# Shifting the weight pieces that stream through TensorE by 48 bytes against their activations

## The chip, the core and the metric

The kernel runs on one core of a Trainium2 chip. The metric is device time in microseconds (us) of one execution. All matrix work is on TensorE (PE), which loads a stationary operand of up to 128x128 (the profile's engine PEld) and then streams a moving operand through the array (PE). VectorE (DVE) and ScalarE (ACT) prepare operands, SyncE (SP) issues the DMAs.

## The reference

Two layers of a decoder trunk over one sequence of 256 tokens, width 2048, all in float32. Every sub-layer is a modulation of its input, a mixer or MLP, a gated residual and a layer norm:

```python
for layer in range(DEPTH):                      # DEPTH = 2
    h = x * (1.0 + scale[:, 0, None]) + shift[:, 0, None]
    y = rglru_mixer(h, ...) if mixer == 0 else nsa_mixer(h, ...)
    x = _layer_norm(DN_ALPHA * x + (1.0 + gate[:, 0, None]) * y, ...)
    h = x * (1.0 + scale[:, 1, None]) + shift[:, 1, None]
    y = jnp.square(jax.nn.relu(h @ w1)) @ w2    # w1: 2048 x 8192, w2: 8192 x 2048
    x = _layer_norm(DN_ALPHA * x + (1.0 + gate[:, 1, None]) * y, ...)
```

Layer 0 mixes with a gated linear recurrence (`lru`), layer 1 with block-sparse attention (`nsa`). Scale, shift and gate come from the matrix `ada_w`. Nearly all of the time is in products of 256 token rows with large weight matrices that are read once from HBM.

## The kernel before, in words

A float32 product is made of three float32r matmuls: every operand is split into a high part (rounded to float32r by a ScalarE copy) and a low part (the rest, by a VectorE subtraction), and `mm3` (lines 208 to 212) issues high x high on line 210, high x low on line 211 and low x high on line 212, into one PSUM bank.

Weights come as a stream of 1 MB items. `prefetch` keeps up to six of them in flight in the tile `raw`. `pump` splits an item, two pieces of 512 columns at a time, into the rings `whi` and `wlo` (lines 143 and 144). Each ring has 16 pieces of 2048 bytes per partition; a split waits until the ring has room, that is until `take` has counted old pieces as consumed. Items of kind "a" (`ada_w`) go through the same stream and are reduced by VectorE on line 125.

A piece is used in one of two ways:

- **weights stationary** (`gemm_ws`, `gemm_ws_outer`, and the small product for the attention gates, lines 1075 to 1087): a 128-column slice of the piece is loaded, and 256 columns of activations move. In the trace these are the rows `128*128 128x256` with `g<-s,whi` or `m<-s,whi`; the moving operand is named first. The attention gates load 48 columns at a time, `128*48`.
- **weights moving** (`gemm_as`): a 128x128 block of activations is loaded, and the whole piece, 512 columns, moves. These are the rows `128*128 128x512` with `g<-whi,s` or `g<-wlo,s`. They are the output products of both mixers (384 matmuls each), every `w2` product of the two MLPs (4 times 384 each), and three single products: two value projections of the attention (96 each) and the first quarter of the first `w1` product of layer 1 (96). That makes 384 + 4x384 + 2x96 + 384 + 96 + 4x384 = 4128 matmuls.

The order of the moving products in time is: mixer output of layer 0 (from 297 us), MLP of layer 0 (from 498, 676, 853 and 1028 us), two value projections (after the norm at 1115 us), mixer output and first `w1` quarter of layer 1 (from 1412 us), MLP of layer 1 (from 1624, 1799, 1974 and 2149 us).

Where the operands lie within a partition follows from the sizes of the tiles in their order of allocation: `whi` begins at byte 50304 and `wlo` at byte 83072, both 128 modulo 256, and every piece and every 128-column slice is a multiple of 256 bytes from there. The activations' high and low parts are slices of 4096-byte tiles (`s` in the trace) from byte 146240 on; each of them begins at 64 modulo 256. So where weights move, the moving operand lies 128 - 64 = 64 bytes past the stationary one, modulo 256; where activations move, 64 - 128 = 192. Only the attention gates differ: their stationary slices step by 192 bytes and so pass through 128, 64, 0 and 192. In the attention and in the recurrence gates there are also matmuls on plain float32 operands, which appear as two records each.

Of the kernel before, what the change touches and what calls it, by code (L numbers as in the profile page):

```python
# [10 lines left out]
F32R = mybir.dt.float32r  # L11
# [18 lines left out]

RAW = 6
RING = 16
NS4 = 20
NS2 = 6
LNACT = (0, 2)
# [5 lines left out]
class Item:  # L41
    def __init__(self, kind, src, col=None, then=None, width=2048):
        self.kind, self.src, self.col, self.then, self.width = kind, src, col, then, width
        self.group = 0
        self.done = False
        self.run = None
        self.pieces = {"w": width // 512, "g": 2}.get(kind, 0)


class Builder:  # L50
    def __init__(self, ctx, tc, a, out):
        self.tc, self.nc, self.a, self.out = tc, tc.nc, a, out
        nc = self.nc
        self.const = ctx.enter_context(tc.tile_pool(name="const", bufs=1))
        self.pool = ctx.enter_context(tc.tile_pool(name="work", bufs=1))
        self.psum = ctx.enter_context(tc.tile_pool(name="psum", bufs=1, space=PSUM))
        self.dram = ctx.enter_context(tc.tile_pool(name="dram", bufs=1, space=DRAM))
        self.raw = self.const.tile([128, RAW, 2048], F32, name="raw")
        self.whi = self.const.tile([128, RING, 512], F32R, name="whi")
        self.wlo = self.const.tile([128, RING, 512], F32R, name="wlo")  # L60
        self.now = 0.0
        self.tasks = []
        self.items = []
        self.di = self.pi = 0
        self.cons = self.prod = 0
        self.slot = self.inflight = 0
        self.hold = self.calm = False
        self.behind, self.left = [], 0
        self.arrive = []
        self.uid = 0  # L70


    def t4(self, shape, dtype=F32):
        self.uid += 1
        return self.pool.tile(shape, dtype, name=f"s{self.uid}", tag="s4", bufs=NS4)

# [11 lines left out]

    def set_stream(self, items):
        self.items = items  # L90
        p = 0
        for it in items:
            it.p0 = p
            p += it.pieces
        self.prefetch()

    def prefetch(self):
# [13 lines left out]
    def pump(self):  # L111
        nc = self.nc
        while self.pi < len(self.items):
            it = self.items[self.pi]
            if it.kind == "d":
                self.pi += 1
                continue
            if self.hold or self.arrive[self.pi] > self.now:
                return
            r = it.raw  # L120
            if it.kind == "a":
                if self.calm:
                    return
                with self.queue():
                    nc.vector.scalar_tensor_tensor(r, r, self.one, self.cond, op0=OP.mult, op1=OP.mult, accum_out=it.col)  # L125
            elif it.kind == "raw":
                if not it.run(r):
                    return
            elif it.kind == "p":
                it.run(r)  # L130
            elif it.kind == "n":
                if not it.done:
                    return
            else:
                w = min(1024, it.width)
                s = it.p0 + 2 * it.group
                if s + 2 > self.cons + RING:
                    return
                src = r[:, 1024 * it.group:1024 * it.group + w]
                hi = self.whi[:, s % RING:s % RING + 2, :].rearrange("p a b -> p (a b)")[:, :w]  # L140
                lo = self.wlo[:, s % RING:s % RING + 2, :].rearrange("p a b -> p (a b)")[:, :w]
                with self.queue():
                    nc.scalar.activation(hi, src, AF.Copy)  # L143
                    nc.vector.tensor_tensor(out=lo, in0=src, in1=hi.bitcast(F32), op=OP.subtract)  # L144
                self.prod = s + 2
                it.group += 1
                if 2 * it.group < it.pieces:
                    continue
            self.pi += 1
            self.inflight -= 1  # L150
            self.prefetch()
            if it.then:
                it.then()
# [41 lines left out]

    def piece(self, i):
        self.until(lambda: self.prod > i)
        return self.whi[:, i % RING, :], self.wlo[:, i % RING, :]

    def take(self):  # L200
        self.cons += 1

    def head(self, kind):

        self.until(lambda: self.items[self.pi].kind == kind and not self.items[self.pi].done and self.arrive[self.pi] <= self.now)
        return self.items[self.pi], self.items[self.pi].raw
# [92 lines left out]
def build(ctx, tc, a, out):  # L299
    B = Builder(ctx, tc, a, out)  # L300
# [46 lines left out]
    def ada_items(s, part, tiles=range(16), then=None):  # L347
        its = [Item("a", a["ada"][s, part * 16 + k], col=mods[s][:, part * 16 + k:part * 16 + k + 1]) for k in tiles]
        if then:
            its[-1].then = then  # L350
        return its
# [6 lines left out]
    def W(name, *ix):  # L358
        return Item("w", a[name][ix])

    def N(name, *ix):
        return Item("n", a[name][ix])

    def merge(main, side):
        res, j = [], 0
        for i, m in enumerate(main):
            res.append(m)
            while j < len(side) and (j + 1) * len(main) <= (i + 1) * len(side):
                res.append(side[j])
                j += 1  # L370
        return res + side[j:]
# [3 lines left out]
    def hook(key):  # L375
        return lambda: hooks[key]()
# [52 lines left out]
    lru_in = [N("lru_gate", 0), N("lru_gate", 1)]  # L429
    for c in (2, 3):  # L430
        lru_in += [W("lru_in", 4 + c, g) for g in range(4)] + [W("lru_in", c, g) for g in range(4)] + [N("lru_gate", c)]
    lru_out = [W("lru_out", n, g) for n in range(4) for g in range(4)]
    def ss_group(k0, k1):
        ks = range(k0, k1)
        return ada_items(1, 0, ks) + ada_items(1, 1, ks, hook(("h1", k0, k1)))
# [9 lines left out]
    def mlp_items(l):  # L445
        its = []
        for q in range(4):
            its += [W("mlp_w1", l, 4 * q + i, g) for i in range(4) for g in range(4)]
            its += [W("mlp_w2", l, n, 4 * q + g) for n in range(4) for g in range(4)]
        return its  # L450

    m0 = mlp_items(0)
    stream += merge(m0[16:], ada_items(1, 2, then=hook(("gate", 1))) + ada_items(2, 0) + ada_items(2, 1, then=hook(("ss", 2))) + ada_items(2, 2, then=hook(("gate", 2))))
    nsa = []
    for ch in (4, 5, 0, 1, 2, 3):
        if ch == 4 or ch == 5:
            idx = {4: 3, 5: 5}[ch]
        else:
            idx = (0, 1, 2, 4)[ch]
        nsa += [W("nsa_kv", idx, g) for g in range(4)]  # L460
    nsa.append(Item("g", a["nsa_g"], width=768))
    cmp_raw = [Item("raw", a["cmp_w1"][i]) for i in range(4)]
    q_items = [W("nsa_q", c, g) for c in range(4) for g in range(4)]
    for i, at in enumerate((18, 21, 24, 27)):
        nsa.insert(at, cmp_raw[i])
    nsa += q_items + [W("nsa_out", n, g) for n in range(4) for g in range(4)]
    stream += merge(nsa, ada_items(3, 0) + ada_items(3, 1, then=hook(("ss", 3))))
    m1 = mlp_items(1)
    stream += m1[:16] + merge(m1[16:96], ada_items(3, 2, then=hook(("gate", 3)))) + m1[96:]

# [606 lines left out]
    gbank = B.bank([128, 256], "g")  # L1077
    whi, wlo = B.piece(B.cons)
    B.until(lambda: B.prod > B.cons + 1)
    ghi = B.whi[:, B.cons % RING:B.cons % RING + 2, :].rearrange("p a b -> p (a b)")  # L1080
    glo = B.wlo[:, B.cons % RING:B.cons % RING + 2, :].rearrange("p a b -> p (a b)")
    for k in range(NK):
        ahi, alo = act(k)
        B.mm3(gbank[0:48, :], ghi[:, 48 * k:48 * k + 48], glo[:, 48 * k:48 * k + 48], ahi, alo, k == 0, k == NK - 1)
# [223 lines left out]
```

## Time and profile before

| | us |
|---|---|
| median of 3 runs | 2252.34 (2247.26 to 2256.88) |
| the profiled execution, its own time | 2251.0 |
| its span, first to last instruction | 2249.2 |
| PE busy | 2152.1 (96% of the span) |
| weight loads (PEld) busy | 1923.5 (86%) |
| DVE busy | 1634.6 (73%) |
| ACT busy | 1058.0 (47%) |

A matmul's duration in the profile runs from its issue to the end of its drain, so consecutive matmuls overlap in the rows; what one costs in a dense stretch is the distance from its start to the next one's. "Granted clock" is the share of TensorE's 2.4 GHz that the chip let through: 1.00 is 2.4 GHz, 0.50 is 1.2 GHz. At 2.4 GHz, 256 columns take 106.7 ns and 512 columns 213.3 ns.

### The profile page before, as it was taken

The page shows a single profiled execution, that of the slowest core. Times are in us where ns is not written, and L with a number is a line of the kernel's source. Part 1 is how long each engine was busy: PE and PEld are TensorE (multiplying, and loading weights), DVE is VectorE, ACT ScalarE, POOL GpSimd, SP SyncE. Part 2 cuts the span into 40 slices and gives each one's busy share as a digit, 9 for nine tenths or more (in the row PEclk, how much of TensorE's full clock was granted, in tenths as well). Part 3 has the DMA queues.
Part 4 walks back from the last instruction along what each step waited for, and adds up shares of the span by engine and source line. Part 5 has one row for each costly group of instructions (what it writes and reads, how often), then busy time and mean ns, then how long its engine had stood idle before and what let it go on. Part 6 is the DMA issues. An engine that isn't in the chain of part 4 may idle for free.

```text
span 2249.2 us, 34081 instructions
## 1 busy us (share of the span) xinstructions
PE 2152.1 (96%) x14093; PEld 1923.5 (86%) x14093; DVE 1634.6 (73%) x1959; ACT 1058.0 (47%) x1387; POOL 0.2 (0%) x4
## 2 busy tenths in 40 slices
PE   3799999899999999999999999999999999999997
PEld 3698877898998898898789998788989989988986
DVE  8888888797677676868898688768777554555566
ACT  2355563554544354354353355536544544543541
POOL 0000000000000000000000000000000000000000
PEclk9899999999999999999999999999999999999999
DMA  9988879699888887879599876355888655555671
GB/s 393 414 316 348 337 294 355 263 344 381 321 306 299 303 324 285 317 291 354 198 345 349 341 274 256 108 206 189 290 326 304 217 191 188 197 197 188 213 255 38
DMA packets 98775, 625.02 MB, mean 278 GB/s; under 512 B 10963, under 2 KB 13443, under 8 KB 27452
## 3 DMA queue, kind: packets, MB, share of 16 engines
q1 hardware_dynamic: 98620, 622.85, 74.0%
q8 instruction: 110, 1.80, 0.3%
q14 instruction: 45, 0.37, 0.0%
HBM read 614.36 MB, written 8.45 MB: 277 GB/s over the span
## 4 chain that ended last, share of the span: by engine, by line
PE 84%; DVE 8%; ACT 3%; DMA 2%; issue 2%; SPq 0%; DVEq 0%; ACTq 0%
PE g L211 26%; PE g L212 26%; PE g L210 26%; DVE raw L125 3%; DVE wlo L144 2%; ACT whi L143 1%; DMA raw<-in_lru_in 1%; PE m L1156 1%; PE m L1190 1%; DMA raw<-in_ada 1%; PE g L896 0%; PE m L1182 0%; PE m L398 0%; DMA raw<-in_cmp_w 0%; PE m L1193 0%
## 5 line engine op out<-in xcount | busy, mean ns | idle before, releaser
L144 DVE TENSOR_TENSOR wlo<-raw,whi 128x1024 fp32r<-128x1024 f32 x721 | 868.8, 1222 | 432.6 <-ACT whi L143 431.1
L143 ACT ACTIVATE whi<-raw 128x1024 fp32r<-128x1024 f32 x721 | 753.4, 1057 | 833.4 <-PE g L212 411.3
L210 PE MATMUL g<-s,whi 128*128 128x256 f32 (+1 forms) x2768 | 771.6, 280 | 60.3 <-ACT s L548 59.1
L211 PE MATMUL g<-s,whi 128*128 128x256 f32 (+1 forms) x2768 | 771.3, 279 | 3.2 <-DVE s L549 3.2
L212 PE MATMUL g<-s,wlo 128*128 128x256 f32 (+1 forms) x2768 | 770.7, 279 | 2.3 <-DVE wlo L144 2.3
L210 PEld LDWEIGHTS g<-s,whi 128*128 128x128 f32 (+1 forms) x2768 | 522.4, 189 | 73.3 <-ACT s L548 60.1
L210 PE MATMUL g<-whi,s 128*128 128x512 f32 x1376 | 540.9, 394 | 5.4 <-ACT whi L143 3.4
L211 PE MATMUL g<-wlo,s 128*128 128x512 f32 x1376 | 542.2, 394 | 2.9 <-DVE wlo L144 2.9
L212 PE MATMUL g<-whi,s 128*128 128x512 f32 x1376 | 542.1, 395 | 0.0
L212 PEld LDWEIGHTS g<-s,wlo 128*128 128x128 f32 (+1 forms) x2768 | 522.8, 189 | 6.6 <-DVE wlo L144 5.5
L211 PEld LDWEIGHTS g<-s,whi 128*128 128x128 f32 (+1 forms) x2768 | 523.6, 189 | 5.7 <-DVE s L549 4.7
L125 DVE SCALAR_TENSOR_TENSOR raw<-raw,one,cond 128x2048 f32<-128x2048 f32 x176 | 411.5, 2346 | 62.3 <-DMA raw<-in_ada 61.6
L210 PEld LDWEIGHTS g<-whi,s 128*128 128x128 f32 x1376 | 259.1, 188 | 65.7 <-ACT whi L143 4.3
L211 PEld LDWEIGHTS g<-wlo,s 128*128 128x128 f32 x1376 | 259.2, 188 | 62.9 <-DVE wlo L144 3.9
L212 PEld LDWEIGHTS g<-whi,s 128*128 128x128 f32 x1376 | 259.3, 188 | 55.8 <-DVE s L549 0.9
L210 PE MATMUL m<-s,whi 128*128 128x256 f32 x256 | 70.6, 277 | 0.2 <-ACT whi L143 0.2
L212 PE MATMUL m<-s,wlo 128*128 128x256 f32 x256 | 70.7, 277 | 0.0
L211 PE MATMUL m<-s,whi 128*128 128x256 f32 x256 | 70.7, 277 | 0.0
L507 ACT ACTIVATE s<-s,hB,hA 128x256 f32<-128x256 f32 x32 | 16.7, 592 | 101.3 <-DVE hA L483 75.7
L549 DVE TENSOR_TENSOR s<-t,s 128x512 fp32r<-128x512 f32 x78 | 53.3, 685 | 3.4 <-ACT s L548 3.2
L731 ACT ACTIVATE t<-g 128x512 f32<-128x512 f32 x58 | 34.0, 587 | 33.2 <-PE g L212 33.2
L548 ACT ACTIVATE s<-t 128x512 fp32r<-128x512 f32 x78 | 47.7, 622 | 2.5 <-DVE t L616 2.3
(196 smaller groups left out, 1045.0 us busy)
## 6 DMA issues: line engine op xcount, KB each, us to landing
raw<-in_mlp_w SPq DMA_DIRECT2D x256, 1024.0 KB
raw<-in_ada SPq DMA_DIRECT2D x176, 1024.0 KB
raw<-in_lru_in SPq DMA_DIRECT2D x28, 1024.0 KB
raw<-in_nsa_kv SPq DMA_DIRECT2D x24, 1024.0 KB
raw<-in_gate SPq DMA_DIRECT2D x16, 1024.0 KB
raw<-in_lru_out SPq DMA_DIRECT2D x16, 1024.0 KB
raw<-in_nsa_q SPq DMA_DIRECT2D x16, 1024.0 KB
raw<-in_nsa_out SPq DMA_DIRECT2D x16, 1024.0 KB
```

Source lines behind the costliest of these rows:

```text
L125: nc.vector.scalar_tensor_tensor(r, r, self.one, self.cond, op0=OP.mult, op1=OP.mult, accum_out=it.col)
L143: nc.scalar.activation(hi, src, AF.Copy)
L144: nc.vector.tensor_tensor(out=lo, in0=src, in1=hi.bitcast(F32), op=OP.subtract)
L210: mm(out, lhi, rhi, start=start, stop=False, skip_group_check=True)
L211: mm(out, lhi, rlo, start=False, stop=False, skip_group_check=True)
L212: mm(out, llo, rhi, start=False, stop=stop, skip_group_check=True)
L507: SC.activation(x[:, j, :], x[:, j, :], AF.Identity, scale=hA[s][:, k:k + 1], bias=hB[s][:, k:k + 1])
L548: SC.activation(hi, src, AF.Copy)
L549: V.tensor_tensor(out=lo, in0=src, in1=hi.bitcast(F32), op=OP.subtract)
L731: SC.activation(r2, banks[b], AF.Relu)
L1156: T.matmul(ps, qT[:, h, 128 * t:128 * t + 128], kT[g // 2][:, g % 2, :, 0:K], start=True, stop=True)
L1190: T.matmul(po, vt[br][:, kt, 128 * g:128 * g + 128], pT[:, br, kt], start=first, stop=False)
```

## The change

Both rings become flat tiles of 16 x 512 elements and 64 elements (256 bytes) of room. A piece whose item is marked as moving is stored 12 elements (48 bytes) from the tile's start plus its slot; every other piece lies 64 elements (256 bytes) from there, which is where it was, modulo 256. The tiles behind the rings move by 512 bytes, so they too keep their places modulo 256. For the moving pieces the distance from moving to stationary operand goes from 64 to 112, modulo 256; nothing else changes its distance.

A moving piece therefore overlaps the last 208 bytes of the slot ahead of it. Two rules keep this safe: at each passage from ordinary to moving pieces two slots are skipped (`skip`, stepped over in `take`), and `pump` doesn't split into ordinary slots until the moving piece that ends in them has been consumed. The matmuls, their order and their operands' values stay as they are.

```diff
 RING = 16
+PLACE = 64
+AHEAD = 52
...
-        self.whi = self.const.tile([128, RING, 512], F32R, name="whi")
-        self.wlo = self.const.tile([128, RING, 512], F32R, name="wlo")
+        self.whi = self.const.tile([128, 512 * RING + PLACE], F32R, name="whi")
+        self.wlo = self.const.tile([128, 512 * RING + PLACE], F32R, name="wlo")
...
     def set_stream(self, items):
         self.items = items
-        p = 0
+        p, last, row = 0, False, -1
         for it in items:
+            if it.pieces and it.moving and not last:
+                self.skip |= {p, p + 1}
+                p += 2
+                row += 1
             it.p0 = p
-            p += it.pieces
+            for _ in range(it.pieces):
+                self.off[p] = PLACE - AHEAD if it.moving else PLACE
+                p += 1
+            if it.pieces:
+                last = it.moving
         self.prefetch()
...
                 if s + 2 > self.cons + RING:
                     return
+                old = s + 2 - RING
+                if not it.moving and old >= self.cons and self.off.get(old, PLACE) != PLACE:
+                    return
                 src = r[:, 1024 * it.group:1024 * it.group + w]
-                hi = self.whi[:, s % RING:s % RING + 2, :].rearrange("p a b -> p (a b)")[:, :w]
-                lo = self.wlo[:, s % RING:s % RING + 2, :].rearrange("p a b -> p (a b)")[:, :w]
+                o = self.off[s] + 512 * (s % RING)
+                hi, lo = self.whi[:, o:o + w], self.wlo[:, o:o + w]
...
     def piece(self, i):
         self.until(lambda: self.prod > i)
-        return self.whi[:, i % RING, :], self.wlo[:, i % RING, :]
+        o = self.off[i] + 512 * (i % RING)
+        return self.whi[:, o:o + 512], self.wlo[:, o:o + 512]
 
     def take(self):
         self.cons += 1
+        while self.cons in self.skip:
+            self.cons += 1
...
-    lru_out = [W("lru_out", n, g) for n in range(4) for g in range(4)]
+    lru_out = moving([W("lru_out", n, g) for n in range(4) for g in range(4)])
...
-            its += [W("mlp_w2", l, n, 4 * q + g) for n in range(4) for g in range(4)]
+            its += moving([W("mlp_w2", l, n, 4 * q + g) for n in range(4) for g in range(4)])
+        if l == 1:
+            moving(its[:4])
         return its
```

The same mark is put on the items of the two value projections and of `nsa_out`, and the small product for the attention gates reads its two pieces at `PLACE`.

## Rows read from the trace of the kernel before

**Rows 1.** The page, busy time by engine: us, share of span, instructions.

```profile
PE 2152.1 (96%) x14093; PEld 1923.5 (86%) x14093; DVE 1634.6 (73%) x1959; ACT 1058.0 (47%) x1387; POOL 0.2 (0%) x4
```

**Rows 2.** The page, the chain that ended last: share of the span by engine.

```profile
PE 84%; DVE 8%; ACT 3%; DMA 2%; issue 2%; SPq 0%; DVEq 0%; ACTq 0%
```

**Rows 3.** PE groups by line and shape: count | busy us, mean ns | idle before.

```profile
L210 PE MATMUL g<-s,whi 128*128 128x256 f32 x2752 | 767.1, 280 | 60.3 <-ACT s L548 59.1 <-ACT whi L143 1.2
...
L211 PE MATMUL g<-wlo,s 128*128 128x512 f32 x1376 | 542.2, 394 | 2.9 <-DVE wlo L144 2.9
L212 PE MATMUL g<-whi,s 128*128 128x512 f32 x1376 | 542.1, 395 | 0.0
L210 PE MATMUL g<-whi,s 128*128 128x512 f32 x1376 | 540.9, 394 | 5.4 <-ACT whi L143 3.4 <-ACT s L548 2.1
```

**Rows 4.** Timeline of PE from 1974 us, weights moving: start us, duration us.

```profile
1973.77 0.39 PE L210 MATMUL g<-whi,s 128*128 128x512 f32 x1
...
1989.79 0.39 PE L211 MATMUL g<-wlo,s 128*128 128x512 f32 x1
```

**Rows 5.** The same from 525 us, weights moving.

```profile
525.11 0.40 PE L210 MATMUL g<-whi,s 128*128 128x512 f32 x1
...
535.84 0.40 PE L212 MATMUL g<-whi,s 128*128 128x512 f32 x1
```

**Rows 6.** The same from 1905 us, activations moving.

```profile
1904.75 0.28 PE L210 MATMUL g<-s,whi 128*128 128x256 f32 x1
...
1912.91 0.28 PE L210 MATMUL g<-s,whi 128*128 128x256 f32 x1
```

**Rows 7.** The same from 655 us, activations moving.

```profile
654.77 0.28 PE L211 MATMUL g<-s,whi 128*128 128x256 f32 x1
...
662.89 0.28 PE L211 MATMUL g<-s,whi 128*128 128x256 f32 x1
```

**Rows 8.** Timeline of PE and PEld together, weights moving.

```profile
1974.00 0.39 PE L211 MATMUL g<-wlo,s 128*128 128x512 f32 x1
1974.00 0.19 PEld L212 LDWEIGHTS g<-whi,s 128*128 128x128 f32 x1
1974.22 0.39 PE L212 MATMUL g<-whi,s 128*128 128x512 f32 x1
1974.23 0.19 PEld L210 LDWEIGHTS g<-whi,s 128*128 128x128 f32 x1
```

**Rows 9.** Timeline of PE from 1269 us, attention gates, 48 columns loaded each.

```profile
1268.78 0.28 PE L210 MATMUL g<-s,whi 128*48 128x256 f32 x1
...
1274.10 0.28 PE L212 MATMUL g<-s,wlo 128*48 128x256 f32 x1
```

**Rows 10.** The chain in order of time, recurrence gates (float32): start, us, what.

```profile
227.82 1.73 PE m L896 x8
229.55 1.73 PE g L896 x8
231.28 1.73 PE m L896 x8
```

**Rows 11.** Busy time by window: PE, PEld, DVE, ACT, POOL, clock, DMA share, GB/s.

```profile
56.00:112.00 56.00, 39.91 (x309) 38.93 (x308) 49.55 (x52) 21.20 (x26) 0.00 (x0) 0.85 1.01 415
...
300.00:380.00 80.00, 80.00 (x342) 65.52 (x343) 74.00 (x81) 33.88 (x34) 0.00 (x0) 0.98 0.91 349
500.00:585.00 85.00, 85.00 (x366) 68.86 (x365) 63.43 (x58) 39.45 (x49) 0.00 (x0) 1.00 0.93 363
680.00:762.00 82.00, 82.00 (x353) 66.39 (x353) 60.04 (x55) 31.46 (x31) 0.00 (x0) 1.00 0.82 306
...
1805.00:1885.00 80.00, 80.00 (x351) 65.66 (x350) 39.19 (x36) 31.07 (x30) 0.00 (x0) 1.00 0.56 190
```

**Rows 12.** ACT's longest waits by line: us in total, times, longest.

```profile
ACT whi L143 <- PE g L212: 411.3, 253, 11.3
ACT whi L143 <- PE g L211: 320.5, 208, 3.1
```

**Rows 13.** The chain in order of time, ahead of the first MLP.

```profile
458.06 8.47 DMA raw<-in_ada
...
466.55 2.37 DVE raw L125 x2
```

More of the change, by code (lines that the diff above doesn't have):

```diff
@@ L47, in __init__, with moving @@
         self.pieces = {"w": width // 512, "g": 2}.get(kind, 0)
+        self.moving = False
+def moving(items):
+    for it in items:
+        it.moving = True
+    return items
 class Builder:
@@ L66, in __init__ @@
         self.slot = self.inflight = 0
+        self.skip, self.off = set(), {}
         self.hold = self.calm = False
@@ L459, in build @@
             idx = (0, 1, 2, 4)[ch]
-        nsa += [W("nsa_kv", idx, g) for g in range(4)]
+        its = [W("nsa_kv", idx, g) for g in range(4)]
+        nsa += moving(its) if ch in (4, 5) else its
     nsa.append(Item("g", a["nsa_g"], width=768))
@@ L465, in build @@
         nsa.insert(at, cmp_raw[i])
-    nsa += q_items + [W("nsa_out", n, g) for n in range(4) for g in range(4)]
+    nsa += q_items + moving([W("nsa_out", n, g) for n in range(4) for g in range(4)])
     stream += merge(nsa, ada_items(3, 0) + ada_items(3, 1, then=hook(("ss", 3))))
@@ L1079, in build @@
     B.until(lambda: B.prod > B.cons + 1)
-    ghi = B.whi[:, B.cons % RING:B.cons % RING + 2, :].rearrange("p a b -> p (a b)")
-    glo = B.wlo[:, B.cons % RING:B.cons % RING + 2, :].rearrange("p a b -> p (a b)")
+    go = PLACE + 512 * (B.cons % RING)
+    ghi, glo = B.whi[:, go:go + 1024], B.wlo[:, go:go + 1024]
     for k in range(NK):
```

## The prediction

> **What bounds the kernel now.** I read the page first: PE is busy for 96% of the span [rows 1] and holds 84% of the chain that ended last [rows 2], so time is won or lost on PE. Then I grouped PE's work by shape. Idle time ahead of the 512-column groups is at most 5.4 us a line [rows 3], and in the windows that lie wholly in such work PE is busy all the time [rows 11]. What matters there is the distance between one matmul and the next, which the durations in a group don't show. So I took start times.
>
> Weights moving, from 1973.77 to 1989.79 us there are 71 starts, 70 steps in 16.02 us: **228.9 ns** a step [rows 4]. From 525.11 to 535.84 us there are 47 starts: 10.73/46 = **233.3 ns** [rows 5]. Activations moving: 73 starts, 8.16/72 = **113.3 ns** [rows 6], and elsewhere 70 starts, 8.12/69 = **117.7 ns** [rows 7]. So each shape has a narrow and a wide spacing, both 4.4 ns apart, at the full 2.4 GHz (granted clock 1.00 [rows 11]) and with no change of the addresses modulo 256. The wide one holds in the first two MLP products of layer 0, from 498 and 676 us: 768 matmuls; 366 matmuls in 85 us and 353 in 82 us [rows 11] agree with it, as 351 in 80 us do with the narrow one (a window also counts a matmul or two that straddle its edges). The other 3360 of the 4128 moving-weight matmuls I take as narrow.
>
> Against streaming alone (213.3 ns for 512 columns, 106.7 for 256) the excess is 15.6 or 20.0 ns with moving weights, and 6.6 or 11.0 with moving activations. Beside every matmul a load for the next one runs; it starts with the matmul, at 1974.00 and at 1974.23 against 1974.22 [rows 8]. So two reads of SBUF run side by side, and the change alters their distance modulo 256 for the moving weights alone, from 64 to 112.
>
> **What the moving pieces may gain.** No row has a float32r matmul at a distance that isn't a multiple of 64, so the cost at 112 can't be read; I bound it.
>
> The best end: the float32 matmuls of the recurrence gates stream 256 columns twice in a record, 512 column times, beside a load of 128 columns, and 24 records in 5.19 us take 216.2 ns each [rows 10]. That is 2.9 ns above the 213.3, with no visible price for the load. It would save 228.9 - 216.2 = 12.7 ns a narrow and 17.1 ns a wide matmul.
>
> The value I take is nearer: moving activations in the narrow spacing, which are of the same type. Their 6.7 ns above streaming looks like a fixed price of a float32r matmul, for the attention gates keep it while they load only 48 columns and pass through the distances 192, 0, 64 and 128: 48 starts, 5.32/47 = 113.2 ns [rows 9]. If loading cost something there, a load of a third of the length should be cheaper. With the same price a 512-column matmul stands at 213.3 + 6.7 = **220.0 ns**. The two observed values are then two and three steps of 4.4 ns above it (228.9 and 233.3), and the wide moving activations one step above 113.3. I read the steps as collisions of the two reads, and forecast that the new distance removes them where weights move: 8.9 ns a narrow matmul, 13.3 a wide one.
>
> The worst end: one step is added, as rows 5 have against rows 4: 4.4 ns x 4128 = 18 us of loss. Two steps, as far as the narrow spacing lies above 220.0, would be 37 us.
>
> **Where the gain arrives.** The mixer output of layer 0 (384 matmuls from 297 us) is followed by a norm and by a stage whose chain runs over a DMA of `ada_w` of 8.47 us and its reductions [rows 13]; what PE wins ahead of that it waits for there. I count these 384 at nothing (3.4 us if the stage doesn't hold it back). All later products are followed by PE-bound work. The sum: 768 x 13.3 = 10.2 us, and (3360 - 384) x 8.9 = 26.5 us; together **36.7 us**.
>
> **The other parts of the edit.** The two skipped slots shorten the split's lead from 16 to 14 pieces at each passage to moving weights. A piece is worth 6 x 228.9 = 1.37 us of PE, so the lead falls from about 22 to 19 us. ACT's split waits for PE to free slots for 411.3 + 320.5 us [rows 12], so the ring is full most of the time and 2.7 us less lead is covered; without that cover it would be 2.7 us at each of ten passages, 27 us. The extra wait for an ordinary piece behind moving ones holds it back by one consumed piece, 1.37 us, under the same cover. Behind a split that has to wait stand the VectorE reductions of line 125 and, through `raw`, SP's next DMAs; those are the queues to look at. The two-halves products, which need all 16 pieces at once, follow other moving pieces or begin after a passage, so no skip falls within their 16. ACT and DVE write the same sizes to other addresses; I count nothing. The DMA has to follow: the busiest window with moving weights, 500 to 585 us, has a DMA share of 0.93 at 363 GB/s; 233.3/220.0 of it is 385 GB/s, under the 415 seen at 56 to 112 us [rows 11]. A shortfall would cost a few us there.
>
> So 2251.0 - 36.7 = 2214.3 us for the profiled execution; the median of the runs is 1.3 us above that execution, so **2215 us** (-1.7%).
>
> **A rule against it.** The load and the stream run side by side in rows 8, and the excess in rows 4 and 5 is what I ascribe to their meeting. The Trainium skill, "TensorE: Matmul & The Clock Gate", section "Part 2: What happens when you issue a matmul", says that PE has two independent SBUF read ports, so that loading the next weights doesn't take read bandwidth from the running matmul. By that rule an address can't matter, and the sum would be zero, not 36.7. The trace agrees with it in rows 10, and rows 9 show no effect of distance or load length; rows 4 to 7 show that something other than streaming costs 4.4 ns at a time, which the rule doesn't explain.
>
> **Rivals.**
> 1. *The distance doesn't matter.* The excess belongs to the float32r stream or to the hand-over between matmuls; the narrow and wide spacings would be a timing relation that sets itself. For it: the spacing changes at equal addresses, and rows 9 have one spacing at four distances. Against it: moving activations show that a float32r matmul beside a full load can do with 6.7 ns, where moving weights pay 15.6. Time: 2251, within 2240 to 2263. A change that fails to move the pieces as it says would look the same.
> 2. *Part of it.* One of two steps goes: 4.4 x 3744 = 16.6 us, 2235.
> 3. *Slower: the new place makes the reads meet more often.* Before, every operand starts on a multiple of 64 bytes; after, the moving ones start 48 past one. If a read that straddles two such blocks occupies both, each matmul gets one step more: 233.3 where it was 228.9, 237.8 where it was 233.3. That is 18 us, 2269 to 2271; with two steps 2289. It decides as soon as the steps gained by the distance are fewer than those lost to the straddling.
>
> **How the numbers follow.** The forecast with all that lies down to the best end, 2194 to 2226 us (the low end: 2976 x 12.7 + 768 x 17.1 = 50.9 us, and 384 x 12.7 = 4.9 us if the first product's gain arrives too): 0.46. Part of it, 2226 to 2240: 0.13. No effect: 0.22. Slower: 0.19. A measurement of this kernel tells about 0.5% (11 us) from no change, so faster 0.59, same 0.22, slower 0.19. The range of 2194 to 2262 us leaves the slower case out. Cases of one sign hold most; the likeliest one's own range is 2194 to 2226.
>
> **What would show it.** Right: steps of about 220 ns in the 512-column stretches, 113.3 ns unchanged where activations move, and 512-column products of 384 matmuls in about 84.5 us instead of 87.9 or 89.6. The forecast is wrong if they stay at 228.9 and 233.3 (rival 1), go to 224 to 229 (rival 2) or rise (rival 3); the covers are wrong if PE waits for lines 143 or 144 at the passages to moving weights, or if the stage after a product gives the gain back in waits for DMA. The wide spacing can also come and go in other stretches: every hundred matmuls in it with moving activations cost 0.44 us.

## The result, and the profile after

The changed kernel took **2266.36 us** (2265.78 to 2266.96) against 2251.98 us (2247.26 to 2256.88) of the kernel before: ratio **1.0072**, 95% interval 1.0058 to 1.0087. It is 0.7% slower where 1.7% faster was forecast, and outside the range. The profiled execution took 2265.78 us with a span of 2264.0, 14.8 us more than the span before.

The page of the kernel after, its busy times and its chain by engine, as in [rows 1, 2]:

```profile
PE 2170.5 (96%) x14093; PEld 1940.3 (86%) x14093; DVE 1637.4 (72%) x1959; ACT 1059.5 (47%) x1387; POOL 0.2 (0%) x4
...
PE 85%; DVE 8%; DMA 3%; ACT 2%; issue 2%; SPq 0%; DVEq 0%; ACTq 0%
```

PE is busy for 18.4 us more, with the same 14093 instructions; the chain is PE's as before. So matmuls became dearer, and no other engine got in the way. The longest waits of ACT's split, and those of PE for the two split lines (now 167 and 168; `mm3` is on 237 to 239), say the same. Columns: us in total, times, longest.

```profile
ACT whi L167 <- PE g L239: 404.2, 246, 12.1
ACT whi L167 <- PE g L238: 338.2, 206, 3.2
...
PE g L237 <- ACT whi L167: 4.3, 3, 3.4
PE g L238 <- DVE wlo L168: 2.9, 2, 1.6
PE g L239 <- DVE wlo L168: 2.3, 4, 0.7
```

PE's waits for the split in the kernel before, where the split lines were 143 and 144:

```profile
PE g L210 <- ACT whi L143: 4.6, 3, 3.4
...
PE g L211 <- DVE wlo L144: 2.9, 2, 1.6
PE g L212 <- DVE wlo L144: 2.3, 4, 0.7
```

ACT waits 742.4 us for PE, against 731.8 [rows 12]: the ring is as full as it was. PE waits 4.3, 2.9 and 2.3 us for the split, against 4.6, 2.9 and 2.3 before.

Which matmuls? Windows of 80 us that lie wholly inside one kind of work, first three of the kernel before, then four of the kernel after. The count behind PE's busy time is the reading: 80 us divided by it (less one or two that straddle the edges) is the step from one matmul to the next.

```profile
857.00:937.00 80.00, 80.00 (x352) 65.62 (x351) 60.41 (x57) 31.15 (x30) 0.00 (x0) 1.00 0.82 304
945.00:1025.00 80.00, 80.00 (x709) 80.00 (x708) 56.21 (x51) 40.49 (x48) 0.00 (x0) 1.00 0.83 310
1716.00:1796.00 80.00, 80.00 (x709) 80.00 (x708) 46.78 (x44) 40.30 (x47) 0.00 (x0) 1.00 0.69 248
```

```profile
1635.00:1715.00 80.00, 80.00 (x354) 66.24 (x354) 58.17 (x51) 35.72 (x39) 0.00 (x0) 1.00 0.86 320
860.00:940.00 80.00, 80.00 (x348) 64.90 (x347) 59.65 (x58) 30.96 (x30) 0.00 (x0) 1.00 0.81 303
950.00:1030.00 80.00, 80.00 (x682) 80.00 (x681) 54.90 (x50) 39.21 (x46) 0.00 (x0) 1.00 0.79 294
1725.00:1805.00 80.00, 80.00 (x681) 80.00 (x681) 44.91 (x43) 39.90 (x47) 0.00 (x0) 1.00 0.65 229
```

The last two windows are the loss: where activations move, whose addresses did not change, 709 matmuls in 80 us became 682, the wide step of [rows 7] instead of the narrow one of [rows 6]. The granted clock is 1.00 in all of them. The first two windows of the kernel after show weights moving, 354 and 348 in 80 us: again a narrow and a wide step. Their sizes come from the timeline of PE, the first and last start of a stretch of 72 and one of 71 matmuls:

```profile
1639.81 0.39 PE L239 MATMUL g<-whi,s 128*128 128x512 f32 x1
...
1655.90 0.39 PE L238 MATMUL g<-wlo,s 128*128 128x512 f32 x1
```

```profile
859.77 0.39 PE L238 MATMUL g<-wlo,s 128*128 128x512 f32 x1
...
875.95 0.40 PE L239 MATMUL g<-whi,s 128*128 128x512 f32 x1
```

16.09/71 = **226.6 ns** and 16.18/70 = **231.1 ns**. Against the 228.9 and 233.3 of [rows 4, 5] each is 2.2 ns lower. So the new place does take time off both, but a quarter of what was forecast, and the wide step, 4.4 ns more, now holds in most stages. Below, "narrow" and "wide" are these two for either kind of work; the wide step is 4.4 ns above the narrow one in both.

From first start to first start of the next stage, in us, for the stages of the two MLPs that alternate (768 matmuls of `w1` with stationary weights, 384 of `w2` with moving ones; the last column is a kernel of the experiments, told there). N and W mark narrow and wide stages, NW a mixed one. The stages of e17 that a small matmul follows include it; the sums are of unrounded times:

| stage | before | after | e17 |
|---|---|---|---|
| `w2`, layer 0, first | 89.6 W | 87.0 N | 87.3 N |
| `w1`, second quarter | 88.7 NW | 90.6 W | 88.3 NW |
| `w2` | 89.6 W | 88.8 W | 87.3 N |
| `w1`, third | 87.1 N | 90.5 W | 87.2 N |
| `w2` | 87.9 N | 88.8 W | 87.3 N |
| `w1`, fourth | 87.1 N | 90.5 W | 87.2 N |
| `w2`, layer 1, first | 87.9 N | 87.0 N | 87.3 N |
| `w1`, second quarter | 87.1 N | 90.5 W | 90.6 W |
| `w2` | 87.9 N | 88.8 W | 87.3 N |
| `w1`, third | 87.1 N | 90.5 W | 87.2 N |
| `w2` | 88.0 N | 88.9 W | 87.5 N |
| `w1`, fourth | 87.1 N | 87.0 N | 87.2 N |
| `w2`, last | 87.7 N | 86.8 N | 86.8 N |
| sum, `w2` (moving weights) | 618.6 | 616.0 | 610.8 |
| sum, `w1` (moving activations) | 524.0 | 539.4 | 527.6 |

The moving weights give 2.6 us, the moving activations cost 15.4. Over the whole kernel, summing the distances from each matmul to the next, the moving weights stand at 969.6 us before and 969.5 after, the moving activations at 1080.5 and 1094.9, all the rest at 148.2 and 148.3. These two totals are quoted for every run below.

The stages change their spacing at the passages between the two kinds of work. The passage from `w2` to `w1` at 587 us before and at 585 us after:

```profile
586.94 0.39 PE L212 MATMUL g<-whi,s 128*128 128x512 f32 x1
587.17 0.28 PE L210 MATMUL g<-s,whi 128*128 128x256 f32 x1
587.29 0.29 PE L211 MATMUL g<-s,whi 128*128 128x256 f32 x1
587.41 0.28 PE L212 MATMUL g<-s,wlo 128*128 128x256 f32 x1
...
588.55 0.28 PE L210 MATMUL g<-s,whi 128*128 128x256 f32 x1
```

```profile
585.37 0.40 PE L239 MATMUL g<-whi,s 128*128 128x512 f32 x1
585.60 0.28 PE L237 MATMUL g<-s,whi 128*128 128x256 f32 x1
585.72 0.28 PE L238 MATMUL g<-s,whi 128*128 128x256 f32 x1
585.84 0.28 PE L239 MATMUL g<-s,wlo 128*128 128x256 f32 x1
...
587.01 0.28 PE L237 MATMUL g<-s,whi 128*128 128x256 f32 x1
```

Before, three steps of about 120 ns and then 113: from 587.41 to 588.55 are ten steps, 114 ns each. After, 117 ns goes on: 585.84 to 587.01 in ten steps. In these two traces all six such passages end narrow before, whether the `w2` stage ahead was wide or narrow; after, five of six end wide. The spacing of `w1` is carried into the next `w2` stage in both kernels.

The mixed stage of the kernel before, from 587 us, has a switch in it that is the kernel's own: one matmul of 128 columns amid the stage. The matmul, and windows on either side of it:

```profile
635.93 0.27 PE L522 MATMUL m<-ident,g 128*16 128x128 f32 x1
```

```profile
594.00:634.00 40.00, 40.00 (x356) 40.00 (x354) 32.74 (x32) 20.35 (x25) 0.00 (x0) 1.00 0.89 340
640.00:674.00 34.00, 34.00 (x291) 34.00 (x290) 24.65 (x22) 15.96 (x19) 0.00 (x0) 1.00 0.77 289
```

The steps, from start to start, are 113.3 ns ahead of it and 117.8 behind it, and the next `w2` stage is wide. In the kernel after, the same matmul stands in a stage that is wide already and leaves it so.

### The profile page after: what moved, and what is told of

Read it like the earlier page. It is cut to its first block, busy times and chain, and to the rows that moved or that the text cites. A ratio compares the mean times of both kernels' runs of the same rounds, so it can differ in the third digit from the quotient of the medians.

```text
span 2264.0 us, 34065 instructions
## 1 busy us (share of the span) xinstructions
PE 2170.5 (96%) x14093; PEld 1940.3 (86%) x14093; DVE 1637.4 (72%) x1959; ACT 1059.5 (47%) x1387; POOL 0.2 (0%) x4
## 4 chain that ended last, share of the span: by engine, by line
PE 85%; DVE 8%; DMA 3%; ACT 2%; issue 2%; SPq 0%; DVEq 0%; ACTq 0%
PE g L239 26%; PE g L238 26%; PE g L237 26%; DVE raw L146 3%; DVE wlo L168 2%; DMA raw<-in_lru_in 2%; ACT whi L167 1%; PE m L1220 1%; PE m L1186 1%; PE m L237 1%; PE m L238 0%; PE m L239 0%; PE m L1212 0%; PE g L926 0%; PE m L1223 0%
```

## Experiments

The theories to tell apart: **place** (where the moving pieces lie makes the difference), **ring** (the skipped slots and the new rules do), and then, within place, whether the loss comes out of the steps at a place or out of the spacing that the passages leave.

**The edit without the shift, and the shift for every piece.** In e1 the moving pieces lie 256 bytes ahead of the others, which is the old place modulo 256, with every new rule kept:

```diff
-AHEAD = 52
+AHEAD = 64
```

> The moving pieces lie 256 bytes ahead of the ordinary ones, so every distance modulo 256 is that of before (64 and 192), while the skipped slots, the extra wait and the flat rings are those of the change. Theory 'place' (the distance sets the moving step, and with it the pattern that the following stage falls into): steps of 228.9 and 233.3 ns with moving weights, narrow 113.3 ns in the stages after them, time of before, 2247 to 2257 us. Theory 'ring' (the skipped slots and the wait shift the schedule and bring the wide pattern): moving steps as before, but 117.7 ns in most stages with moving activations, about 2270 to 2276 us, since the 9 us that the moving steps win are missing.

In e2 all pieces lie 48 bytes further and nothing is marked as moving, so no slot is skipped; the loads of `w1` slices move too, to distance 144:

```diff
-PLACE = 64
-AHEAD = 52
+PLACE = 12
+AHEAD = 0
```

> All pieces, ordinary and moving, lie 48 bytes further, with no skipped slots and no extra wait: distance 112 where weights move, as after the change, and 144 instead of 192 where activations move. Theory 'place': moving steps of 226.7 (narrow) or 231.1 (wide) ns as after the change; where activations move, a spacing that differs from 113.3 and 117.7 would show that the distance counts there too, the same two spacings that it doesn't. Theory 'ring': no wide stretches beyond those of before, 226.7 ns with moving weights, about 2242 us.

e1: 2252.52 us, ratio 1.0012 (1.0002 to 1.0022); totals 968.6 and 1079.5. e2: 2297.57 us, ratio 1.0214 (1.0199 to 1.0229); totals 971.9 and 1124.5. The windows with moving activations, e1 first, then e2:

```profile
1893.00:1973.00 80.00, 80.00 (x709) 80.00 (x707) 38.52 (x35) 40.03 (x47) 0.00 (x0) 1.00 0.55 188
```

```profile
1925.00:2005.00 80.00, 80.00 (x669) 80.00 (x668) 37.44 (x34) 39.23 (x46) 0.00 (x0) 1.00 0.54 182
```

The ring theory falls: the rules cost 0.1% (0.2% at most, by the interval), and the loss is the place's. And e2 shows a step that neither kernel has: 669 in 80 us, 119.8 ns, with the activations where they were and only the loaded slices moved. The place of the loaded operand matters too, although loads of 48 columns at four places had shown nothing [rows 9].

**Is it chance?** The two kernels once more, unchanged:

> The changed kernel once more, for a second trace. Theory 'place': the same stages are narrow and wide as in the first trace (wide with moving activations after 5 of the 6 MLP products of moving weights that such a stage follows), 2264 to 2268 us. Theory 'lottery' (each execution draws its patterns anew): other stages wide, time off by up to 10 us.

> The kernel before once more, for a second trace. Theory 'place': every stage with moving activations that follows an MLP product of moving weights settles at 113.3 ns within a few matmuls, as 6 of 6 did in the first trace; wide stretches only where a stall stands ahead of them, so 2246 to 2258 us. Theory 'lottery': wide stages in other and in more places.

After again: 2268.56 us. The same five `w1` stages are wide, and the counts of narrow and wide steps with moving weights (by the mean of three steps) are the same to within a few, about 1416 and 2546 in both traces.

Before again: 2249.0 us, and here not everything comes back, against the expectation. The windows of [rows 11] from 500 us, and one in the `w1` stage behind the first passage:

```profile
500.00:585.00 85.00, 85.00 (x373) 69.75 (x372) 64.96 (x59) 39.56 (x50) 0.00 (x0) 1.00 0.93 366
590.00:635.00 45.00, 45.00 (x384) 45.00 (x384) 36.24 (x33) 23.34 (x29) 0.00 (x0) 1.00 0.84 316
```

The first `w2` stage is narrow, 373 matmuls where the first trace had 366, and so is the second (87.9 us each), while the mixer output ahead of them is wide (233.3 ns) and was narrow; the passage at 587 us ends wide, and the kernel's own matmul, at 637.63 us, turns that stage narrow. So one program can differ from execution to execution up to some 676 us; behind that the `w1` and `w2` stages of the two traces agree.

The loss is not chance all the same. The four times of the kernel after lie within 1.2 us, and five of six passages are wide in both of its traces; at the old place 17 of 18 are narrow (before, before again and e1).

**Other places.** Only `AHEAD` differs: 56, 48, 32, 16 and 20 instead of 52.

> Moving pieces 32 bytes further instead of 48: distance 96 where weights move. Theory 'distance modulo 256' (the step depends on the distance itself): a step of its own, between 226.7 and 228.9 ns in the narrow pattern. Theory 'blocks of 64' (what counts is that the two operands no longer start at the same place within 64 bytes): the same 226.7 and 231.1 as at 112. Which stationary stages turn wide is open in both; if the place left behind at the passage decides, it need not be the same ones as after the change. 2240 to 2275 us.

> Moving pieces 64 bytes further: distance 128. Theory 'distance modulo 256': a step other than 228.9 is likely. Theory 'blocks of 64': 228.9 and 233.3 as before, narrow stages as before, 2247 to 2257 us.

> Moving pieces 128 bytes further: distance 192, what the moving activations have in every kernel. Theory 'distance modulo 256': moving weights reach the same price per column as they have, 226.7 ns narrow. Theory 'blocks of 64': 228.9 and 233.3, time of before.

> Moving pieces 192 bytes further: distance 0, moving and stationary operand at the same place modulo 256. Distances so far, narrow pattern: 228.9 ns at 64, 226.7 at 112, and 231.7 to 233.8 at 96, 128 and 192. Theory 'distance modulo 256': a step of its own, at least 226.7 (one part in 16 above streaming). Theory 'only 112 of those tried is free': 231 to 234 ns, so 10 to 20 us more than before where the stationary stages stay narrow.

> The moving pieces lie 176 bytes further, at distance 240. If a 512-column step follows the distance's nearness to 0 (226.7 at 0), it is 226.7 to 229; if it follows the distance modulo 64 (48, as with 112, where it is 226.7 and 231.1), the levels are 226.7 and 231.1 again; if neither, 233. No forecast of the total beyond 2250 to 2285.

The windows with moving weights at distance 96 (e5), 0 (e12) and 240 (e16):

```profile
1830.00:1910.00 80.00, 80.00 (x344) 64.36 (x343) 38.68 (x36) 29.80 (x28) 0.00 (x0) 1.00 0.54 188
```

```profile
1810.00:1890.00 80.00, 80.00 (x354) 66.26 (x354) 40.52 (x38) 32.75 (x33) 0.00 (x0) 1.00 0.56 196
```

```profile
1825.00:1905.00 80.00, 80.00 (x340) 64.39 (x339) 38.55 (x35) 29.56 (x30) 0.00 (x0) 1.00 0.53 184
```

354 in 80 us against 340: a spread of 4% with nothing changed but the place. At 240 the step is as dear when the splits and the DMA are over: the last split of e16 ends at 2247.6 us, and behind it the DMA's share is 0.00.

```profile
2248.00:2264.00 16.00, 16.00 (x69) 12.86 (x69) 9.88 (x21) 0.30 (x1) 0.00 (x0) 1.00 0.00 0
```

```profile
2248.78 0.40 PE L238 MATMUL g<-wlo,s 128*128 128x512 f32 x1
...
2262.27 0.40 PE L238 MATMUL g<-wlo,s 128*128 128x512 f32 x1
```

58 starts, 13.49/57 = 236.7 ns, as amid the stream: neither the split's writes, whose place moved with the pieces, nor the DMA's are needed for the dearer step. All of it, with the time of the kernel before on the same chip in brackets; before and after are medians of four, the others one execution each:

| distance | kernel | step of 512 columns, ns | moving weights, us | moving activations, us | time, us |
|---|---|---|---|---|---|
| 0 | e12 | 226.7 | 961.4 | 1102.4 | 2264.72 (2249.78) |
| 64 | before | 228.9, 233.3 | 969.6 | 1080.5 | 2251.98 |
| 96 | e5 | 233.3 | 985.0 | 1098.4 | 2285.3 (2257.07) |
| 112 | after | 226.7, 231.1 | 969.5 | 1094.9 | 2266.36 (2251.98) |
| 128 | e6 | 232.4 on average, 228 to 241 | 982.6 | 1080.9 | 2264.62 (2257.07) |
| 192 | e7 | 233.3 on average, 230 to 236 | 985.2 | 1080.8 | 2267.82 (2257.07) |
| 240 | e16 | 236.7 on average, 234 to 240 | 998.2 | 1081.1 | 2281.97 (2251.94) |

Three readings. First, most expectations were missed: 192 is not one of the good places, 96 is dearer than either theory had it, 0 is not dear, and at 240 none of the three values came out. At 64 and 112 the moving weights have two spacings; at 0, 96, 192 and 240 the `w2` stages of these traces have one, whatever the `w1` stage ahead. Nor does the distance modulo 64 order the steps: 0 and 112 share the best one, 0, 64, 128 and 192 do not agree. Second, the two totals do not go together: the best places for moving weights, 0 and 112, have dear `w1` stages, and 128, 192 and 240 have cheap ones. Third, at 0 all six passages inside the MLPs end wide, at 128 one of them, at 192 and 240 none.

**The price by columns.** In e11 two products of `w2` in layer 1 multiply 384 of the 512 columns and leave the rest of the product out:

```diff
+                    n = 384 if self.cut and k else 512
+                    self.mm3(b[t][:, :n], ahi, alo, whi[:, :n], wlo[:, :n], k == 0, k == NK - 1)
```

> The changed kernel, in which two of the MLP products of layer 1 (the second and third of w2) multiply only 384 of each piece's 512 columns in all but the first of 16 pieces, so a quarter of these products is left out. Asks what the 6.7 ns above streaming are: a price per matmul gives 160.0 + 6.7 = 166.7 ns for 384 columns in the narrow pattern; a price per column, one part in 16, gives 160.0 x 17/16 = 170.0 ns; the wide pattern 4.4 ns more in both. These two stretches shorten by about 60 x 90 ns x 4 = 21 us each, so 2220 to 2228 us.

The run took 2230.4 us. First and last start of a stretch of 57 matmuls:

```profile
1822.14 0.33 PE L238 MATMUL g<-whi,s 128*128 128x384 f32 x1
...
1831.85 0.33 PE L240 MATMUL g<-whi,s 128*128 128x384 f32 x1
```

The 384-column matmuls take 173.3 ns, in a sequence of 171, 176, 175, 175, 169 and 174. Neither expectation holds. Streaming alone is 160.0, so the excess is 13.3 ns, and so it is in the narrow 512-column step at this place, 226.7 - 213.3. Whether these stretches were narrow or wide can't be told, since no kernel shows 384 columns in both; so a price per column is not excluded by this.

**Disturbing the passages.** If only the pattern that a passage leaves is at fault, something small between the stages should change it, at the same addresses. e8 is the changed kernel with small float32 matmuls at six places, one to two of 16, 64 or 128 columns, whose results nobody reads; e13 is the same kernel again, in 12 runs and with a trace of its own.

```diff
+            if q:
+                cols, times = KICK[l][q - 1]
+                kb = B.bank([128, 512], "m")
+                for _ in range(times):
+                    T.matmul(kb[0:16, 0:cols], condT, ident[:, 0:cols], start=True, stop=True)
```

> The changed kernel with one or two small float32 matmuls (16, 64 or 128 columns, into an unused bank, result not read) ahead of each stage with moving activations that follows moving weights inside an MLP; six passages, in layer 0 one each of 16, 64 and 128 columns, in layer 1 two each of 128, 16 and 64. Theory 'passage' (the relative timing that the moving weights leave behind decides which pattern the next stage locks into): the addresses being those of the change, a disturbance at the passage turns several of the five wide stages narrow, 113.3 instead of 117.7 ns, 2.6 to 3.4 us each (576 to 768 matmuls x 4.4 ns); moving weights stay at 226.7 or 231.1. Rival 'address' (the wide pattern in those stages is a property of the new layout itself): all five stay wide, about 2267 us.

> The kernel of the look with six small matmuls of three sizes, now timed in rounds. Theory 'passage': as in that look, five of six stationary stages narrow, so about 13 us under the changed kernel's 2266, 2250 to 2255 us, and no more than 0.2% from before. If the look was one lucky execution, the runs scatter up to 2266.

e8: 2252.77 us, totals 965.1 and 1085.4. e13: 2252.51 us, ratio **0.9999** (0.9986 to 1.0012): the loss is gone. The first small matmul was not issued at its passage but amid the `w2` stage ahead, at 509.4 us, so that in e8 the passage at 588 us had none. The windows behind that passage and behind the next one, at 767 us, which had one:

```profile
592.00:672.00 80.00, 80.00 (x682) 79.99 (x681) 60.60 (x58) 39.83 (x48) 0.00 (x0) 1.00 0.81 303
...
770.00:850.00 80.00, 80.00 (x708) 80.00 (x707) 58.17 (x54) 39.96 (x47) 0.00 (x0) 1.00 0.81 302
```

Wide where nothing was put, as in the kernel after; narrow where a single matmul of 64 columns was put, and at the four other passages too. But in e13, the same program, the passage at 590 us, with nothing put there either, ended narrow:

```profile
594.00:634.00 40.00, 40.00 (x355) 40.00 (x354) 32.73 (x30) 19.96 (x23) 0.00 (x0) 1.00 0.85 324
```

So what the `w2` stage ahead hands over counts, and not the place alone. The misplaced one is the clearest case. The timeline around it in e8, and the stretch behind it, from 514 to 585 us, in e8 and in e13:

```profile
500.51 0.40 PE L238 MATMUL g<-whi,s 128*128 128x512 f32 x1
...
508.60 0.40 PE L240 MATMUL g<-whi,s 128*128 128x512 f32 x1
...
509.39 0.21 PE L757 MATMUL m<-ident,condT 128*16 128x16 f32 x2
```

```profile
514.00:585.00 71.00, 71.00 (x315) 58.80 (x314) 53.72 (x48) 32.86 (x40) 0.00 (x0) 1.00 0.96 381
```

```profile
514.00:585.00 71.00, 71.00 (x309) 57.60 (x308) 53.98 (x48) 33.62 (x40) 0.00 (x0) 1.00 0.95 374
```

In e8 the stage ran wide ahead of it (36 starts from 500.51 to 508.60: 231.1 ns) and narrow behind it: 315 matmuls in 71 us, and 226.7 ns from start to start. In e13, where the stage ran narrow (36 starts in 7.94 us, 226.9 ns), the same small matmul turned it wide: 309 in 71 us, and 231.1 ns from start to start. One product, one set of addresses, both spacings, and 16 columns of foreign work between them.

Then small matmuls pinned to every passage: e9 with eleven of 16 columns, e10 the same on the kernel before, e14 with ten of 64.

```diff
+    def kick(self):
+        kb = self.bank([128, 512], "m")
+        with self.tc.issue_after(self.last.ins):
+            self.nc.tensor.matmul(kb[0:16, 0:16], self.kin[0], self.kin[1], start=True, stop=True)
```

> The changed kernel with eleven small float32 matmuls (16 columns, result not read), each held behind the last matmul ahead of it: at every passage from moving to stationary weights inside the MLPs and after the two single products, at the start of both mixers' output products, and 33 matmuls into the first MLP product. Theory 'passage': nearly all long stretches narrow, 226.7 ns with moving weights and 113.3 with moving activations. Against before: 4128 x 2.2 = 9.2 us less for the distance, up to 7 us less for the wide stretches that before has, 11 x 0.35 = 3.9 us more for the small matmuls: about 2238 to 2244 us where before has 2250. Rival 'address': the stationary stages stay wide, 2264 to 2270 us.

> The kernel before with the same eleven small matmuls. Theory 'passage': narrow nearly everywhere, 228.9 and 113.3 ns, 7 us less and 3.9 us more than before, about 2246 to 2250 us; the distance alone is then the difference to the run with the change and the small matmuls, 9 us. If the small matmuls did something else than choose the pattern (free a wait, say), it would gain as much as the other run does.

> The changed kernel with ten small matmuls of 64 columns, each held in place: the six passages inside the MLPs, the two behind single products, one 33 matmuls into the first w2 product and one before the last w1 part of the second MLP quarter. Theory 'passage': if nearly all long stretches come out narrow, 2250 - 9.2 (distance) - up to 7 (before's own wide stretches) + 10 x 0.4 = 2238 to 2245 us, below before. If the first products of layer 0 stay wide as with 16 columns (4.4 ns x some 1500), 2246 to 2252 us.

e9: 2255.62 us, ratio 1.0028 (1.0018 to 1.0037), totals 969.4 and 1082.6. e10: 2252.52 us, ratio 1.0015 (1.0006 to 1.0025), totals 968.9 and 1079.6. e14: 2252.93 us, ratio 1.0002 (0.9989 to 1.0015), totals 969.3 and 1078.7. On the changed kernel the small matmuls take back 10 to 16 us by the ratios; on the kernel before they cost 2.7 us. But the times hoped for were missed in all three: e10 stayed above its 2246 to 2250, e9 came out 3.1 us slower than e10 on the same chip, not 9 faster, and e14 missed 2238 to 2245. With moving weights about half of the steps stayed wide (about 1815 narrow and 2140 wide in e9, 2200 and 1755 in e14), so that the 2.2 ns that the place gives don't show in the total.

**The place without wide `w2` stages.** At distance 0 the `w2` stages were narrow by themselves and all `w1` stages wide. So: distance 0 (`AHEAD = 16`) with nine small matmuls, of 64 columns in e15, 16 in e17, 128 in e18.

> The moving pieces lie at distance 0 from their activations, and nine small 64-column matmuls stand behind moving stages. Theory 'the passages set the pattern': moving stages stay narrow, 961 to 964 us in all (1102.4 and 961.4 at this distance without the small matmuls), stationary-weight stages return to narrow, 1079 to 1083 us; the small matmuls cost 9 x 0.42 = 3.8 us; the time is 2241 to 2249 against 2250 of the kernel before. Rival 'the distance 0 makes stationary stages wide whatever stands at the passage': 1095 to 1102 us there, the time 2262 to 2268.

> As with nine small matmuls at distance 0, but of 16 columns instead of 64. Theory 'the phase left by the passage decides': another length leaves another phase, so at least some of the six passages inside the MLPs turn narrow; with all of them, stationary-weight stages 1079 to 1083 us and the time 2242 to 2248. Rival 'distance 0 makes the next stage wide whatever precedes it': 1098 to 1102 us and 2262 to 2268.

> The same with 128 columns. The two theories expect the same alternatives as with 16 columns: 1079 to 1083 us and 2243 to 2249 if all six passages turn narrow, 1098 to 1102 us and 2262 to 2268 if none does.

| kernel | columns | `w1` stages behind the six passages | moving weights, us | moving activations, us | time, us | ratio |
|---|---|---|---|---|---|---|
| e15 | 64 | six wide (one in part) | 961.0 | 1099.9 | 2264.99 | 1.0060 (1.0042 to 1.0078) |
| e17 | 16 | five narrow (one in part), one wide | 960.1 | 1079.9 | **2243.03** | **0.9969** (0.9959 to 0.9980) |
| e18 | 128 | six wide (one in part) | 961.3 | 1104.4 | 2268.73 | 1.0079 (1.0064 to 1.0095) |

The windows behind one and the same passage, near 1885 us, in e17 and in e18, and the one exception in e17, from 1705 us:

```profile
1885.00:1965.00 80.00, 80.00 (x708) 80.00 (x707) 38.01 (x34) 40.23 (x47) 0.00 (x0) 1.00 0.54 190
1705.00:1785.00 80.00, 80.00 (x682) 80.00 (x681) 46.08 (x44) 40.01 (x47) 0.00 (x0) 1.00 0.65 237
```

```profile
1905.00:1985.00 80.00, 80.00 (x682) 80.00 (x681) 37.03 (x34) 38.40 (x46) 0.00 (x0) 1.00 0.51 178
```

e15 missed its forecast and, with e18, has the times of the rival; e17 is inside the other theory's range. The stages marked "in part" are the second quarter of layer 0, which has the kernel's own matmul of 128 columns and one of the nine small ones in it: in e17 the kernel's own turned it wide at 631 us and the small one narrow again at 649 us.

Neither "the place decides alone" nor "any disturbance helps" survives: at the same place, 16 columns leave the narrow spacing and 64 or 128 the wide one. And e17 is faster than both kernels: 9.5 us less with moving weights than the kernel before, 0.6 less with moving activations, 1.1 more in the rest. A small matmul of 16 columns delays the stage by about 0.33 us: four steps of 318, 39, 106 and 222 ns where 234 and 117 stand without it.

## Why the prediction was wrong, point by point

**What bounds the kernel** was right, and so was the reading of two spacings in each kind of work. The covers held as well: e1 has the ring's rules at 0.1%, PE's waits for lines 167 and 168 did not grow, and at 500 to 585 us the DMA delivered 374 GB/s at a share of 0.95 while PE ran at the narrow 226.7.

**The floor of 220.0 ns** failed. It carried the 6.7 ns of moving activations over to moving weights as a fixed price of the type. No place of seven had a mean step below 226.7, and 384 columns have 13.3 ns above streaming as well. The excess of moving weights is not the excess of moving activations plus removable collisions.

**"The steps of 4.4 ns are collisions that the distance removes"** is the step that failed most, and the rows ahead of it spoke against it: both spacings at equal addresses [rows 4 to 7]. The 4.4 ns are a pattern that a stage keeps and that something as small as 16 foreign columns switches (e8, e13). The 768 matmuls that the sum took as wide were wide in one execution only: in the second trace of the same kernel they are narrow. What the place changes directly is another, smaller thing: 2.2 ns in either pattern, where 8.9 and 13.3 were in the sum. Even with every `w2` stage narrow, as in e17, the gain with moving weights is 9.5 us, not the 36.7 of the sum.

**The term that was left at nothing** is the one that set the sign. The sum has no line for moving activations, since their addresses don't change; the last sentence on the signs to look for priced a hundred such matmuls in the wide spacing at 0.44 us and went no further. Four `w1` stages of 768 that were narrow turned wide, 3.4 us each, and a fifth, half wide before, lost 1.9: 15.4 us with the sixth, as the table shows. A pattern known to be carried over long stretches [rows 6, 7] should have had a rival of its own: up to 4.4 ns for each matmul with moving activations.

**The first 384 at nothing**: from their start to that of the first `w2` stage there are 200.4 us before, 203.0 after and 199.2 in e17. Their own stage was wide after the change, and where it was narrow, in e17, the stretch is 1.2 us shorter. Of that, 384 x 2.2 ns = 0.8 us at most is this product's own saving: small, but not nothing.

**The rivals.** The slower one had the sign and nearly the time (2269 to 2271 against 2266, with a chance of 0.19), but for a reason that the runs refute: it put one step more on every moving matmul, and their total is unchanged at 969.5; and the cost does not follow pieces that start off a multiple of 64 bytes, for 128 and 192 are dearer per step than 112. "The distance doesn't matter" had the other half: the spacing does set itself, and yet the place matters, both for the step and for what the passage leaves.

**The rule.** By the Trainium skill, "TensorE: Matmul & The Clock Gate", section "Part 2: What happens when you issue a matmul", two independent read ports let a load run beside a matmul without taking its bandwidth. The runs disagree with what the prediction drew from it, that an address can't matter: 354 against 340 matmuls in 80 us at distances 0 and 240, and 119.8 instead of 113.3 ns in e2, where of the two operands only the loaded slices had moved. They don't show whether it is the ports that meet.

**What stays open.** What in the engine holds the pattern; whether the distance counts or the place itself, since the activations were never moved; and why one passage in e17 stayed wide, and the one at 587 us in the second trace of the kernel before. That a small matmul acts through the time that it takes would fit e15, e17 and e18, but no run varied that time alone.

## What to carry to other kernels

Where a tuned matmul stream is 96% busy, read the start-to-start distance stage by stage, before and after: a layout change can move the spacing of stages that it doesn't touch. Do not add up removable steps until one row shows a step with the cause removed; two values at equal addresses can be a pattern that keeps itself, and it can also go the other way. Take a second trace of the same program before building on which stage has which spacing: here the first stages differed. A candidate place is judged together with the passages that follow it: here distance 0 was 8 us faster or 13 to 18 us slower than the kernel before, by the length of a small matmul between two stages.

## What the runs showed of the hardware

- A float32r matmul of 512 columns beside a load of 128 columns has a step of 226.7 ns (distances 0 and, narrow, 112) to 236.7 (240), by where its operand lies modulo 256; with 256 columns, 113.3 or 117.7 ns at distance 192 and 119.8 at 144.
- At some places the step has two lasting patterns 4.4 ns apart: with moving weights at 64 and 112, with moving activations at 192. They last hundreds of matmuls and, at 64 and 112, go over from moving activations into moving weights. They are switched in either direction by one matmul of 16 columns (231.1 to 226.7 in e8, 226.9 to 231.1 in e13), and by the kernel's own of 128 (113.3 to 117.8 before, 117.8 to 113.3 in its second trace). From one execution of a program to another they repeat in most stages, but not in all.
